# Moving ScalarE's pieces for the turned results, the down half's first cast and the bank copies within their queues, in a one-core decoder layer

## The chip, the cores and the metric

The kernel runs on one core of one Trainium2 chip. The metric is the device time of one execution in microseconds. The core has a matrix engine (TensorE, PE in the profile, its weight loads PEld), VectorE (DVE), ScalarE (ACT), GpSimd (POOL) and SyncE (SP), each with a queue of its own that is worked off in the order in which the program was written; semaphores join the queues. Matmuls write eight banks of PSUM, 512 float32 columns each.

## The reference

One decoder layer for 256 tokens with a model width of 2048, all in float32. The part that this change touches is the feed-forward:

```python
D_FF = -(-8 * D_MODEL // (3 * 256)) * 256          # 5632
...
    f = rmsnorm(h, ffn_norm[i])
    h = h + (jax.nn.silu(f @ w_gate[i]) * (f @ w_up[i])) @ w_down[i]
```

Ahead of it stand the attention of two head groups and their output projection, behind it a gate on per-layer embeddings and the final norm. None of these changes.

## The kernel before

**Splitting.** Every matmul operand is split in two: a high part, which ScalarE makes by a cast (L338, `split_hi`), and a low part, the rest, which VectorE makes by a subtraction (L349, `split_lo`). A product is three matmuls (`three`, L389 to L391): high times high, low times high, high times low. Weights arrive in raw tiles by SyncE's transfers (five buffers, `raw_112` to `raw_2909` in the rows below) and their parts go into places of `ring`, `more` and `most`, which come free when TensorE has read them.

**Stages.** The 5632 columns of the feed-forward are done in five blocks of 1024 and one of 512. For block n there are a gate gn (`gate`), then the first half of the down product of the block before, then the up product un, then the second half of the down product. In this text d2, d3 and d4 are the first halves that follow g2, g3 and g4 (`d20`, `d30`, `d40` in the code). gu5 is the last, short block, and `dl0` the down half behind it.

**Units.** A gate or up product is eight units of 256 weight rows. Seven of them, S0 to S6, are done with seven products in place of eight (`seven`, Strassen's scheme). Such a unit has four turns, each with a job of its own: the first quarter pair ("11 22", 1024 columns wide), the second quarter ("21", 512), the sums "t1 t3" (1024, here called the third quarter) and "t4 t2" (1024, the fourth). The sums are made in the raw tile by VectorE (L348, L351, L352) between the low parts, so the casts of the third and fourth quarter wait for VectorE. In g2 to g4 the order is unit 7 first, then S0 to S6; a down half is four units, each cast at once (2048 columns).

**The gate's end.** In the last unit of a gate ScalarE copies the finished banks into the tile `stage` (`gate_add`, L1027), four copies, and one of Strassen's products into U (L467). The banks go over to the down half behind it, in the order of the copies, so its first matmul waits for the first copy. VectorE adds up U from the other products (L474 to L477), and POOL adds U to `stage` by a transfer (`gate_sum`). At the end of a down half ScalarE copies its banks into `copied` (L945), and the up product's first matmuls take them over.

**The turned results.** `ff_transpose` turns the result of an up product (TensorE at L1065, ScalarE's copies at L1069) into the left operand of the down half that follows the next gate. Its parts are made by `by_transfer`, a task of four pieces during that gate: two high parts by ScalarE's casts (L1089, `ffTh`), then two low parts, each a negated copy by ScalarE (L1092, `ffTl`) and an accumulating transfer that POOL issues (L1093). A task goes a step on at every second turn (`step`).

**What sets the order.** The program is written out by the loop at the end: for each turn of each unit it collects the jobs whose raw tile and place are free by the plan (`todo`), lets `high_parts` write their casts, steps the tasks, writes the low parts and then the matmuls. No scheduler changes this order afterwards.

Of the kernel before, what the change touches and what calls it, by code (L numbers as in the profile page):

```python
# [35 lines left out]
def kernel(ctx, tc, x, w_in, w_ukv, w_o, w_gate, w_up, w_down, w_ple_gate, w_ple_proj,  # L36
                             final_norm, x_turned, p_turned, columns_in, out):
    nc = tc.nc
# [130 lines left out]
    units = []  # L169
# [61 lines left out]
    jobs, turns = [], []  # L231
# [99 lines left out]
    def split_hi(jb, c0=0, c1=None, n=1, row=slice(None)):  # L331

        jb.cast = c1 is None
        h, l, r = (x[:, row] for x in by_row_tile(n, *parts_of(jb), raw_of(jb)))
        if units[jb.unit].adding:
            nc.scalar.mul(l, r, -1.0)
            nc.gpsimd.dma_start(l, r, accum_op=ALU.add)
        nc.scalar.copy(h[:, :, c0:c1], r[:, :, c0:c1])  # L338

    def split_lo(jb, c0=0, c1=None, n=1, row=slice(None)):  # L340

# [104 lines left out]
    def seven(u, turn):  # L446
        st = u.st
        if turn == 0 and u.sevens_first:
            take_banks(u)
            n = B["next"] % 4  # L450
            st["free"] = B["rot"][n:] + B["rot"][:n]
            B["rot"], B["next"] = [st["banks"][1, 1]] if u.first else [], 0
            st.update(zip(("m1", "m7", "m5", "m6"), st["free"]))
        h, l = u.turns[turn][0].h, u.turns[turn][0].l
        k = u.ks[0]
        a11, a12, a22 = u.lhs(k, 0), u.lhs(k + 1, 0), u.lhs(k + 1, 1)
        s1, s2, s3, s4 = (u.sums(k, j) for j in range(4))
        todo = (((0, "m1", a11), (1, "m3", s4)), ((0, "m2", a12),), ((1, "m7", s3), (0, "m5", s1)),
                ((1, "m6", s2), (0, "m4", a22)))[turn]
        alone = {"m2": (0, 0), "m3": (1, 0), "m4": (0, 1)}  # L460
        for q, m, xs in todo:
            b = st["banks"][alone[m]] if m in alone else st[m]
            three(b, xs, h[:, 512 * q:512 * q + 512], l[:, 512 * q:512 * q + 512], begins(u, alone.get(m, m)),
                  u.sevens_end and (u.last or m not in alone))
        if u.sevens_end and turn == (0 if u.last else 3):
            S["U"] = big.tile([128, NT, 1024], F32, name="U", tag="vb")
            nc.scalar.copy(S["U"][:, 0, 0:512], st["m1"])  # L467
        for c, t in (((1, 1), (1, 0)), ((0, 0),), (), ((0, 1),))[turn] if u.last else ():
            u.evac(c, t, *u.chunks[c], st["banks"][c, t])
        if turn == 3 and u.sevens_end:  # L470
            U = S["U"]
            c1, c2 = U[:, :, 0:512], U[:, :, 512:1024]
            tt = nc.vector.tensor_tensor
            tt(c2[:, 0], c1[:, 0], st["m6"], op=ALU.add)  # L474
            tt(c1[:, 1], c2[:, 0], st["m7"], op=ALU.add)
            tt(c2[:, 0], c2[:, 0], st["m5"], op=ALU.add)
            tt(c2[:, 1], c1[:, 1], st["m5"], op=ALU.add)  # L477
            B["rot"], B["next"] = st["free"], 0
            if u.last:
                gate_sum()  # L480
                B["acc"] = [st["banks"][ct] for ct in ((1, 1), (1, 0), (0, 0), (0, 1))]
            if u.into is not None:
                def join(hs=S["h"][:, :, u.into:u.into + 1024]):
                    tt(hs, hs, U, op=ALU.add)
                    yield 1
                add(join())
# [28 lines left out]
    def add(gen, wait=0, front=False):  # L515
        tasks.insert(0 if front else len(tasks), [wait, gen])
# [72 lines left out]
    turn = {"P": 0, "pT": 0}  # L589
# [464 lines left out]
    def ff_transpose(ci, n, st):  # L1054
        if ci == 5:
            ft = big.tile([128, 2, 6, SEQ], F32R, name="ffT", tag="att")
            tl = ffT[ci] = [ft[:, 0], ft[:, 1]]
        else:
            tl = ffT[ci] = parts_tile("ffT", "f0")
        lows = []  # L1060
        for k in range(0, n // 128, 2):
            b = obank()
            for i in range(2):
                for t in range(NT):
                    nc.tensor.transpose(b[:, (2 * i + t) * 128:(2 * i + t + 1) * 128],  # L1065
                                        st[:, t, (k + i) * 128:(k + i + 1) * 128], ident)
            h, l, f = tl[0][:, k:k + 2, :], tl[1][:, k:k + 2, :], b.rearrange("q (a s) -> q a s", a=2)
            if ci in (1, 2, 3, 4):
                nc.scalar.copy(st[:, :, k * 128:(k + 2) * 128], f)  # L1069
            elif ci or k < 4:  # L1070
                split_psum(h, l, f)
            else:
                kept = st[:, :, k * 128:(k + 2) * 128]
                nc.scalar.copy(kept, f)
                lows.append((l, kept, h))
                nc.scalar.copy(h, kept)
            if k % 4 == 2:
                yield 1

        def low_parts():  # L1080
            for l, kept, h in lows:
                nc.vector.tensor_tensor(l, kept, h.bitcast(F32), op=ALU.subtract)
            yield 1

        def by_transfer():
            v = st.rearrange("q a (m s) -> q m a s", s=SEQ)
            h, l = (x.rearrange("q (m a) s -> q m a s", a=2) for x in tl)
            for a in range(2):
                nc.scalar.copy(h[:, :, a], v[:, :, a])  # L1089
                yield 1  # L1090
            for a in range(2):
                nc.scalar.mul(l[:, :, a], v[:, :, a], -1.0)  # L1092
                nc.gpsimd.dma_start(l[:, :, a], v[:, :, a], accum_op=ALU.add)  # L1093
                yield 1
        if lows:
            add(low_parts(), 11, True)
        elif ci < 5:
            add(by_transfer(), 2)

    def ff_l(k, t):  # L1100
        ci, kk = divmod(k, 8)
# [216 lines left out]
    for n in range(3):  # L1318
        for i in range(4):
            if n:  # L1320
                u = Unit()
# [26 lines left out]
        split_lo(jobs[1], c0, c1)  # L1348
    add(prologue(), 1)

    def high_parts(todo):

        ahead = [jb for jb in todo if not (jb.kind in ("t1 t3", "t4 t2") and any(
            x.unit == jb.unit and x.kind in ("11 22", "21") for x in todo))]
        for jb in ahead:
            if not jb.cast:
                split_hi(jb)

# [14 lines left out]
    def may_wait(i, jb):  # L1373
        return i in (end_u0 - 1, end_u0) and (
            jb.unit > end_u0 + 2 or jb.unit == end_u0 + 2 and jb.kind in ("t1 t3", "t4 t2"))

    for i, u in enumerate(units):
# [32 lines left out]
        for n in range(max(1, len(u.turns))):  # L1410
# [3 lines left out]
            while nxt < len(jobs) and jobs[nxt].unit in raw and jobs[nxt].wait < j and jobs[nxt].unit <= i + (3 if i > 1 else 1) and \  # L1414
                    (jobs[nxt].unit <= i + 2 or i >= wide and units[jobs[nxt].unit].asked < i) and \
                    not (u.sevens_end and u.name != "u0" and 0 <= n < 3 and jobs[nxt].unit > i + 1) and \
                    not may_wait(i, jobs[nxt]):
                todo.append(jobs[nxt])
                nxt += 1
            weave = u.name in WOVEN and u.last  # L1420
# [63 lines left out]
```

## Time and profile before

| | |
|---|---|
| median of 3 runs | 1191.82 us (1191.62 to 1191.92) |
| the profiled execution, its own time | 1192.29 us |
| its span, first to last instruction | 1190.3 us |
| mean granted TensorE clock | 0.995 |
| casts of weights into `ring`, `more`, `most` (L338, ACT) | 377.1 + 85.4 + 58.8 us |
| low parts of the same (L349, DVE) | 442.5 + 98.9 + 69.1 us |
| sums in the raw tiles (L348, L352, DVE) | 69.8 + 39.4 us |

The times of one engine add up along its queue; those of different engines lie beside each other. A number in square brackets behind a row of a timeline is the time for which the engine stood idle before it, with what ended this. A row with x3 holds three instructions that follow each other. In the list of waits the numbers are us in all, times, and the longest.

### The profile page before, as it was taken

The page shows a single profiled execution, that of the slowest core. Times are in us where ns is not written, and L with a number is a line of the kernel's source. Part 1 is how long each engine was busy: PE and PEld are TensorE (multiplying, and loading weights), DVE is VectorE, ACT ScalarE, POOL GpSimd, SP SyncE. Part 2 cuts the span into 40 slices and gives each one's busy share as a digit, 9 for nine tenths or more (in the row PEclk, how much of TensorE's full clock was granted, in tenths as well). Part 3 has the DMA queues.
Part 4 walks back from the last instruction along what each step waited for, and adds up shares of the span by engine and source line. Part 5 has one row for each costly group of instructions (what it writes and reads, how often), then busy time and mean ns, then how long its engine had stood idle before and what let it go on. Part 6 is the DMA issues. An engine that isn't in the chain of part 4 may idle for free.

```text
span 1190.3 us, 14715 instructions
## 1 busy us (share of the span) xinstructions
PE 1169.5 (98%) x5459; PEld 975.9 (82%) x5459; DVE 980.4 (82%) x1167; ACT 737.9 (62%) x939; POOL 61.0 (5%) x82
## 2 busy tenths in 40 slices
PE   9999999999999999999999999899989999999996
PEld 7888888899888888888887888688878888888886
DVE  7866656875567779999989998999899989898984
ACT  6745745457466655767666766667576667465563
POOL 5000000000000000000000000000000000000000
PEclk9999999999999999999999999999999999999999
DMA  9896886755675686787978697878778797936441
GB/s 331 284 350 214 289 298 235 277 181 213 242 288 176 241 285 243 270 268 251 303 200 272 187 339 224 248 210 323 235 201 255 262 299 196 376 117 238 155 165 70
DMA packets 90103, 291.99 MB, mean 245 GB/s; under 512 B 5808, under 2 KB 12208, under 8 KB 85424
## 3 DMA queue, kind: packets, MB, share of 16 engines
q1 hardware_dynamic: 76208, 238.66, 55.6%
q0 software_dynamic: 13248, 51.38, 16.7%
q10 hardware_dynamic: 576, 1.02, 0.3%
q8 instruction: 42, 0.69, 0.2%
q14 instruction: 29, 0.24, 0.1%
HBM read 252.24 MB, written 26.21 MB: 234 GB/s over the span
## 4 chain that ended last, share of the span: by engine, by line
PE 92%; DVE 3%; ACT 2%; issue 2%; DMA 0%; ACTq 0%; DVEq 0%; SPq 0%
PE bank L391 29%; PE bank L389 29%; PE bank L390 29%; DVE ringl L349 1%; PE bank L602 1%; PE bank L1065 1%; ACT ringh L338 1%; PE bank L123 1%; ACT moreh L338 1%; PE bank L631 1%; PE bank L625 0%; PE bank L737 0%; PE bank L605 0%; DVE raw L348 0%; DVE raw L352 0%
## 5 line engine op out<-in xcount | busy, mean ns | idle before, releaser
L338 ACT CAST ringh<-raw 128x1024 fp32r<-128x1024 f32 (+4 forms) x322 | 377.1, 1205 | 237.1 <-PE bank L390 82.5
L349 DVE TENSOR_TENSOR ringl<-raw,ringh 128x1024 fp32r<-128x1024 f32 (+5 forms) x319 | 442.5, 1407 | 87.1 <-ACT ringh L338 85.4
L389 PE MATMUL bank<-ringh,aT 128*128 128x512 f32 (+3 forms) x688 | 264.8, 385 | 0.5 <-ACT copied L945 0.5
L391 PE MATMUL bank<-ringl,aT 128*128 128x512 f32 (+3 forms) x688 | 260.8, 379 | 0.1
L390 PE MATMUL bank<-ringh,aT 128*128 128x512 f32 (+3 forms) x688 | 260.4, 378 | 0.0
L389 PEld LDWEIGHTS bank<-ringh,aT 128*128 128x128 f32 x688 | 129.4, 188 | 24.8 <-ACT copied L945 1.3
L391 PEld LDWEIGHTS bank<-ringl,aT 128*128 128x128 f32 x688 | 129.2, 188 | 24.2 <-DVE ringl L349 0.8
L390 PEld LDWEIGHTS bank<-ringh,aT 128*128 128x128 f32 x688 | 129.4, 188 | 22.7 <-DVE aT L669 0.2
L338 ACT CAST moreh<-raw 128x1024 fp32r<-128x1024 f32 (+2 forms) x78 | 85.4, 1127 | 46.0 <-DVE raw L348 29.8
L349 DVE TENSOR_TENSOR morel<-raw,moreh 128x1024 fp32r<-128x1024 f32 (+2 forms) x77 | 98.9, 1304 | 10.8 <-ACT moreh L338 10.2
L338 ACT CAST most<-raw 128x1024 fp32r<-128x1024 f32 (+2 forms) x58 | 58.8, 1036 | 28.7 <-DVE raw L348 15.6
L389 PE MATMUL bank<-ringh,ffTh 128*128 128x512 f32 x180 | 71.0, 394 | 2.0 <-ACT stage L1027 2.0
L348 DVE TENSOR_TENSOR raw<-raw 128x1024 f32<-128x1024 f32 x57 | 69.8, 1225 | 2.0
L349 DVE TENSOR_TENSOR most<-raw,most 128x1024 fp32r<-128x1024 f32 (+2 forms) x58 | 69.1, 1202 | 2.2 <-ACT most L338 1.9
L391 PE MATMUL bank<-ringl,ffTh 128*128 128x512 f32 x180 | 70.8, 393 | 0.0
L390 PE MATMUL bank<-ringh,ffTl 128*128 128x512 f32 x180 | 70.6, 392 | 0.0
L389 PEld LDWEIGHTS bank<-ringh,ffTh 128*128 128x128 f32 x180 | 34.2, 190 | 9.5 <-ACT stage L1027 2.4
L389 PE MATMUL bank<-moreh,aT 128*128 128x512 f32 x105 | 41.3, 393 | 0.0
L352 DVE TENSOR_TENSOR raw<-raw 128x512 f32<-128x512 f32 x57 | 39.4, 692 | 2.0
L391 PE MATMUL bank<-morel,aT 128*128 128x512 f32 x105 | 40.9, 390 | 0.0
L390 PE MATMUL bank<-moreh,aT 128*128 128x512 f32 x105 | 40.9, 389 | 0.0
L390 PEld LDWEIGHTS bank<-ringh,ffTl 128*128 128x128 f32 x180 | 34.2, 190 | 7.1
(379 smaller groups left out, 2053.4 us busy)
## 6 DMA issues: line engine op xcount, KB each, us to landing
raw<-in_w_down SPq DMA_DIRECT2D x44, 1024.0 KB, 6.5
raw<-in_w_gate SPq DMA_DIRECT2D x37, 1024.0 KB, 8.4
raw<-in_w_up SPq DMA_DIRECT2D x30, 1024.0 KB, 5.9
raw<-in_w_in SPq DMA_DIRECT2D x40, 512.0 KB, 5.2
raw<-in_w_o SPq DMA_DIRECT2D x16, 1024.0 KB, 5.9
raw<-in_w_ple_gate SPq DMA_DIRECT2D x16, 1024.0 KB, 5.1
wsums<-in_w_up POOLq DMA_DIRECT2D x10, 1024.0 KB, 7.5
wsumsu<-wsums POOLq DMA_DIRECT2D x10, 1024.0 KB, 4.7
```

Source lines behind the costliest of these rows:

```text
L123: nc.tensor.transpose(b[:, (2 * i + t) * 128:(2 * i + t + 1) * 128], part[:, t, i * 128:(i + 1) * 128], ident)
L338: nc.scalar.copy(h[:, :, c0:c1], r[:, :, c0:c1])
L348: tt(f[:, 0:2], f[:, 1:2].to_broadcast([128, 2, 512]), f[:, 0:4:3], op=ALU.subtract)
L349: tt(l[:, :, c0:c1], r[:, :, c0:c1], h[:, :, c0:c1].bitcast(F32), op=ALU.subtract)
L352: tt(f[:, 2], f[:, 2], f[:, 3], op=ALU.subtract)
L389: nc.tensor.matmul(b, xh, h, start=start, stop=False)
L390: nc.tensor.matmul(b, xl, h, start=False, stop=False)
L391: nc.tensor.matmul(b, xh, l, start=False, stop=stop)
L602: nc.tensor.matmul(s[:, c0:c0 + nk], qT[:, q * 128:(q + 1) * 128], kT[:, 0:nk], start=True, stop=qpe is None)
L631: nc.tensor.matmul(o[:, 0:256], v(0), pT[:, 0:256], start=True, stop=False)
L1065: nc.tensor.transpose(b[:, (2 * i + t) * 128:(2 * i + t + 1) * 128], st[:, t, (k + i) * 128:(k + i + 1) * 128], ident)
```

## The change

```diff
@@ split_hi
         nc.scalar.copy(h[:, :, c0:c1], r[:, :, c0:c1])
+        if jb.kind != "21":
+            return
+        if pieces:
+            pieces.pop(0)()
+
+    pieces = []
@@ seven
-        if u.sevens_end and turn == (0 if u.last else 3):
+        for c, t in (((1, 1), (1, 0)), ((0, 0),), (), ((0, 1),))[turn] if u.last else ():
+            u.evac(c, t, *u.chunks[c], st["banks"][c, t])
+        if u.sevens_end and turn == (1 if u.last else 3):
             S["U"] = big.tile([128, NT, 1024], F32, name="U", tag="vb")
             nc.scalar.copy(S["U"][:, 0, 0:512], st["m1"])
-        for c, t in (((1, 1), (1, 0)), ((0, 0),), (), ((0, 1),))[turn] if u.last else ():
-            u.evac(c, t, *u.chunks[c], st["banks"][c, t])
@@ by_transfer
-            for a in range(2):
-                nc.scalar.copy(h[:, :, a], v[:, :, a])
-                yield 1
-            for a in range(2):
+            def low(a):
                 nc.scalar.mul(l[:, :, a], v[:, :, a], -1.0)
                 nc.gpsimd.dma_start(l[:, :, a], v[:, :, a], accum_op=ALU.add)
-                yield 1
+            def high(a):
+                nc.scalar.copy(h[:, :, a], v[:, :, a])
+            pieces.extend([partial(low, 0), partial(low, 1), partial(high, 0), partial(high, 1)])
...
         elif ci < 5:
-            add(by_transfer(), 2)
+            by_transfer()
@@ the loop
+    def behind_run(i, n=1):
+        return i >= wide and units[i].idx == n - 1 and units[i - n].strassen
+
+    def held(i, jb):
+        u = units[jb.unit]
+        if u.strassen and u.last and jb.kind in ("t1 t3", "t4 t2"):
+            return next(x for x in jobs[nxt:] if x.unit == jb.unit + 1).wait >= j
+        return any(behind_run(jb.unit, n) for n in (2, 3)) and i < jb.unit - 2
@@ high_parts
-        for jb in ahead:
+        for jb in sorted(ahead, key=lambda x: not behind_run(x.unit)):
@@ the loop's condition for a job
-                    not may_wait(i, jobs[nxt]):
+                    not may_wait(i, jobs[nxt]) and not held(i, jobs[nxt]):
```

The four pieces of the turned results are no longer a task: each is written right behind the next cast of a second quarter, the low ones first. The third and fourth quarter of a gate's last unit are held back until the first unit of the down half has its place by the plan, and that unit's cast is written ahead of theirs; the casts of the second and third unit of the down half are held back until two units ahead. In the last unit the bank copies are written before the copy to U, which goes a turn later. The order on TensorE, on POOL and on SyncE is the same as before, and no instruction is added or taken away.

ScalarE's queue in g3 where S4 (`raw3`) and S5 (`raw4`) are cast. Before:

```order
L338 CAST ringh_115<-raw3_2907 128x1024
L338 CAST ringh_115<-raw3_2907 128x512
L1092 ACTIVATE ffTl_5082<-stage_4519 128x4x256
L338 CAST ringh_115<-raw3_2907 128x1024 x2
L1092 ACTIVATE ffTl_5082<-stage_4519 128x4x256
L338 CAST ringh_115<-raw4_2909 128x1024
L338 CAST ringh_115<-raw4_2909 128x512
L338 CAST ringh_115<-raw4_2909 128x1024
```

With the change:

```order
L338 CAST ringh_115<-raw3_2907 128x1024
L338 CAST ringh_115<-raw3_2907 128x512
L1100 CAST ffTh_5081<-stage_4514 128x4x256
L338 CAST ringh_115<-raw3_2907 128x1024 x2
L338 CAST ringh_115<-raw4_2909 128x1024
L338 CAST ringh_115<-raw4_2909 128x512
L1100 CAST ffTh_5081<-stage_4514 128x4x256
L338 CAST ringh_115<-raw4_2909 128x1024
```

The piece between S4's fourth quarter and S5's first has gone behind S5's second quarter; the two low pieces have moved up to S2 and S3.

ScalarE's queue at the end of g3: S6 (`raw0`), then the four units of d3 (`raw1` to `raw4`). Before:

```order
L338 CAST most_3392<-raw0_112 128x512
L338 CAST most_3392<-raw0_112 128x1024
L338 CAST ringh_115<-raw0_112 128x1024
L338 CAST ringh_115<-raw1_113 128x2048
L338 CAST ringh_115<-raw2_114 128x2048
L467 COPY U_5320<-bank0_77 128x512
L1027 COPY stage_5322<-bank5_82 128x512
L1027 COPY stage_5322<-bank7_84 128x512
L1027 COPY stage_5322<-bank6_83 128x512
L338 CAST moreh_2523<-raw3_2907 128x2048
L1027 COPY stage_5322<-bank4_81 128x512
L338 CAST most_3392<-raw4_2909 128x2048
```

With the change:

```order
L338 CAST most_3392<-raw0_112 128x512
L338 CAST ringh_115<-raw1_113 128x2048
L338 CAST most_3392<-raw0_112 128x1024
L338 CAST ringh_115<-raw0_112 128x1024
L1033 COPY stage_5317<-bank5_82 128x512
L1033 COPY stage_5317<-bank7_84 128x512
L1033 COPY stage_5317<-bank6_83 128x512
L475 COPY U_5324<-bank0_77 128x512
L338 CAST ringh_115<-raw2_114 128x2048
L1033 COPY stage_5317<-bank4_81 128x512
L338 CAST moreh_2523<-raw3_2907 128x2048
L338 CAST most_3392<-raw4_2909 128x2048
```

The cast of d3's first unit now stands behind S6's second quarter, and the second unit's cast behind the copies.

VectorE's queue at the same place. Before:

```order
L349 TENSOR_TENSOR most_3392<-raw0_112,most_3392 128x1024
L349 TENSOR_TENSOR ringl_116<-raw0_112,ringh_115 128x1024
L349 TENSOR_TENSOR ringl_116<-raw1_113,ringh_115 128x2048
L349 TENSOR_TENSOR ringl_116<-raw2_114,ringh_115 128x2048
L349 TENSOR_TENSOR morel_2524<-raw3_2907,moreh_2523 128x2048
L474 TENSOR_TENSOR U_5320<-U_5320,bank3_80 128x512
```

With the change:

```order
L355 TENSOR_TENSOR most_3392<-raw0_112,most_3392 128x1024
L355 TENSOR_TENSOR ringl_116<-raw0_112,ringh_115 128x1024
L355 TENSOR_TENSOR ringl_116<-raw1_113,ringh_115 128x2048
L355 TENSOR_TENSOR ringl_116<-raw2_114,ringh_115 128x2048
L480 TENSOR_TENSOR U_5324<-U_5324,bank3_80 128x512
L481 TENSOR_TENSOR U_5324<-U_5324,bank2_79 128x512
```

The sums of U stand ahead of the low part of d3's third unit instead of behind it; the order of the other low parts is kept.

## The prediction, made before the change was run

> **What bounds the kernel now.** I read the busy shares first, then TensorE's waits, then the stretches round those waits engine by engine.
>
> ```profile
> PE 1169.5 (98%) x5459; PEld 975.9 (82%) x5459; DVE 980.4 (82%) x1167; ACT 737.9 (62%) x939; POOL 61.0 (5%) x82
> ```
>
> TensorE is busy for 98% of the span, so reordering can bring little over one per cent. What can be had lies where it stands still, and the list of its waits has one cause at the top: three waits of 2.0 us for ScalarE's copies out of the banks (L1027).
>
> ```profile
> PE bank L389 <- ACT stage L1027: 6.0, 3, 2.0
> ```
>
> They stand at the ends of the gates g2, g3 and g4. TensorE's timeline at the end of g3:
>
> ```profile
> 757.16 0.50 PE L391 MATMUL bank<-most,sums6h 128*128 128x512 f32 x1 [1.17 <-DVE most L349]
> ...
> 761.76 0.50 PE L389 MATMUL bank<-ringh,ffTh 128*128 128x512 f32 x1 [2.02 <-ACT stage L1027]
> ```
>
> First it waits for VectorE's low part of the third quarter of S6 (the gate's last unit), then for a bank that d3 wants. Right behind, the clock falls (granted clock is the third number from the end); in g4 it doesn't:
>
> ```profile
> 763.04:766.44 3.40, 3.40 (x10) 2.66 (x9) 2.36 (x2) 3.40 (x3) 0.00 (x0) 0.50 0.98 384
> ...
> 885.89:889.30 3.41, 2.43 (x10) 1.65 (x10) 2.82 (x2) 3.41 (x3) 0.00 (x0) 1.00 0.33 56
> 889.30:892.70 3.40, 2.36 (x10) 1.97 (x11) 2.75 (x2) 3.40 (x6) 0.00 (x0) 1.00 1.00 376
> ```
>
> 3.4 us at half speed lose 1.7 us behind g3, and as much behind g2. In g4 the same wait of 2.0 us is spread over two of these stretches, and nothing is lost.
>
> Why does the low part come late? VectorE's timeline, and ScalarE's below it:
>
> ```profile
> 744.82 1.23 DVE L349 TENSOR_TENSOR ringl<-raw,ringh 128x1024 fp32r<-128x1024 f32 x1 [0.67 <-ACT ringh L338]
> ...
> 750.42 2.36 DVE L349 TENSOR_TENSOR morel<-raw,moreh 128x1024 fp32r<-128x1024 f32 x2
> 752.82 1.23 DVE L348 TENSOR_TENSOR raw<-raw 128x1024 f32<-128x1024 f32 x1
> ...
> 755.89 1.22 DVE L349 TENSOR_TENSOR most<-raw,most 128x1024 fp32r<-128x1024 f32 x1
> 757.16 1.23 DVE L349 TENSOR_TENSOR ringl<-raw,ringh 128x1024 fp32r<-128x1024 f32 x1
> 758.98 4.50 DVE L349 TENSOR_TENSOR ringl<-raw,ringh 128x2048 fp32r<-128x2048 f32 x2 [0.59 <-ACT ringh L338]
> 764.52 2.29 DVE L349 TENSOR_TENSOR morel<-raw,moreh 128x2048 fp32r<-128x2048 f32 x1 [1.04 <-ACT moreh L338]
> ```
>
> ```profile
> 742.79 1.06 ACT L1092 ACTIVATE ffTl<-stage 128x1024 fp32r<-128x1024 f32 x1
> 743.75 1.56 ACT L338 CAST ringh<-raw 128x1024 fp32r<-128x1024 f32 x2
> ...
> 751.24 0.62 ACT L338 CAST most<-raw 128x512 fp32r<-128x512 f32 x1
> 754.16 1.05 ACT L338 CAST most<-raw 128x1024 fp32r<-128x1024 f32 x1 [2.29 <-DVE raw L348]
> 756.09 4.66 ACT L338 CAST ringh<-raw 128x1024 fp32r<-128x1024 f32 x3 [0.88 <-DVE raw L352]
> 760.64 0.58 ACT L467 COPY U<-bank 128x512 f32<-128x512 f32 x1
> 761.12 1.56 ACT L1027 COPY stage<-bank 128x512 f32<-128x512 f32 x3
> ```
>
> Between its bracketed gaps VectorE works without a break: it is **the engine that sets the end of each gate**. A gap of 0.67 arises where ScalarE does a piece for the turned results (1.06 us, L1092) just ahead of the next unit's first cast. The gaps of 0.59 and 1.04 arise because d3's casts come late, the latter behind the bank copies.
>
> **The change part by part.** It adds and removes no instruction, and no DMA: everything is a move on ScalarE, with one on VectorE.
>
> The **pieces** now stand behind the second-quarter cast. There ScalarE waits anyhow: 2.29 us ahead of 754.16 in the row above, for VectorE's L348. A piece of 1.06 us fits in it, so the two gaps of 0.67 in g3 close. The two low pieces go first, so POOL's two accumulating transfers are issued earlier, which nobody waits for; the high ones are done at least a unit ahead of their first use.
>
> The **first cast of d3** goes ahead of S6's third-quarter cast. Moved earlier by 2 x 0.65 us, S6's second-quarter cast ends at 751.86 - 1.35 = 750.5; the moved cast takes 1.9 (the row at 756.09 holds 1.05 and two of these) and ends at 752.4; L348 ends at 754.05 - 1.3 = 752.75. The cover is 0.35 us: later than that, every microsecond of this cast delays VectorE's next low part by one.
>
> The **bank copies** then follow the fourth-quarter cast directly: that cast ends near 755.9, so d3's first bank is free at 756.4 instead of 761.7. The wait of 2.02 goes. What is late next is VectorE: S6's third-quarter low part is ready at 757.1 - 1.3 = 755.8. TensorE wants it at about 755.2 (757.16 less the 1.17 idle and some 0.8 of holds too short for the list), so 0.6 to 0.7 of that wait stays; S6's fourth follows, and d3's first low part (2.29) is ready at 759.4 where TensorE wants it at 758.6: a new wait of 0.8. Then the second d3 cast ends at 759.6, a gap of 0.2 on VectorE, and the **sums of U** go ahead of the third low part, which has time (d3's third unit is 11 us behind its first).
>
> So TensorE could go 2.85 us earlier (d3's third matmul, the one that reads the low part, stood at 762.3 and now at 759.5), and 1.7 more if the clock stays up: 4.5. But VectorE only gains its closed gaps, and ScalarE's casts for u3 follow it. The same rows for the other gates, as sums of waits in 34 and 33 us round their ends, g2 first, then g4:
>
> ```profile
> DVE ringl L349 <- ACT ringh L338: 1.7, 2, 1.1
> DVE most L349 <- ACT most L338: 0.7, 1, 0.7
> DVE morel L349 <- ACT moreh L338: 0.6, 1, 0.6
> ```
>
> ```profile
> DVE ringl L349 <- ACT ringh L338: 1.7, 2, 1.1
> DVE morel L349 <- ACT moreh L338: 0.6, 1, 0.6
> ```
>
> VectorE gains in g2 1.7 + 0.7 + 0.6 - 0.3 = 2.7; in g3 2 x 0.67 + 0.59 + 1.04 - 0.3 = 2.65; in g4 1.7 + 0.6 - 0.4 = 1.9 (only one piece's gap there; the 0.2 to 0.4 is what stays at the second cast). At the end of each down half stands the next check: the copy of its first bank (L945) comes behind casts that follow VectorE, and the next unit wants that bank. ScalarE's copy at d2's end, and TensorE's first matmuls behind d2, d3 and d4:
>
> ```profile
> 654.64 1.55 ACT L945 COPY copied<-bank 128x512 f32<-128x512 f32 x3
> ```
>
> ```profile
> 656.15 0.39 PE L389 MATMUL bank<-ringh,aT 128*128 128x512 f32 x1
> ```
>
> ```profile
> 785.37 0.50 PE L389 MATMUL bank<-ringh,aT 128*128 128x512 f32 x1
> ```
>
> ```profile
> 912.96 0.50 PE L389 MATMUL bank<-ringh,aT 128*128 128x512 f32 x1 [0.55 <-ACT copied L945]
> ```
>
> Behind d2 the copy is done at 655.2, 0.95 before it is wanted; behind d3 it just holds TensorE (a matmul of 0.50 is one that waited), behind d4 it does by 0.55. With the copies earlier by VectorE's gain alone, TensorE gains there at most 2.7 + 0.95 = **3.6** (it could 4.3), **2.65** (it could 4.5: a new wait of 1.9 for L945), **1.9** (it could 2.0). In gu5 two pieces' gaps close likewise, and a hold of 0.2 goes. The sum is 3.6 + 2.65 + 1.9 + 0.2 = **8.3 us**. The u units behind start with VectorE's lead as before: after d3 and d4 both engines move by the same amount; after d2 TensorE moves 0.9 further, which can cost a part of this in u2.
>
> The clock: half of it followed single waits of 2.0 us inside one stretch of 3.4 (g2, g3) and not 1.2 us in one. The new wait of 1.9 lies between. I take no halving, since it must also fall inside one stretch; the other end is 1.7 us. The Trainium skill (TensorE: Matmul & The Clock Gate, "Part 1: The HAM clock gate") lets the clock fall only after an idle window of about 3.4 us. The trace disagrees: waits of 2.0 us were enough. By the trace the halvings go with these waits; by the Trainium skill's rule they had another cause and would stay.
>
> **The rivals.**
>
> *VectorE isn't what sets the pace* behind the gates, and no wait for L945 arises: then TensorE has all that it could gain, 4.3 + 4.5 + 2.0 + 0.2 = 11.0, 1180.8. For it speaks that TensorE's own rows show these losses; against it VectorE's unbroken work from 744.8 to 758.4, and the 0.55 for L945 that is there already.
>
> *Halved clock comes back* behind the new 1.9 us wait: 8.3 - 1.7 = 6.6, 1185.2. Near half of the places at which the wait can fall would put it into one stretch; whether 1.9 is enough no row says.
>
> *The halvings aren't these waits' doing* and stay: that behind g3 hides in the new wait for L945, that behind g2 costs 1.7 less the 0.7 that it hides there, 7.3 in all, 1184.5. Against it: two of two stand right behind a wait of 2.0 in one stretch. The Trainium skill's page on the clock gate would have it so.
>
> *Pieces bring nothing*, as another wait (TensorE's release of ring places) keeps VectorE's gaps: then only the tails count, 0.6 + 1.05 - 0.3 = 1.3 a gate, and 0.95: 3 x 1.3 + 0.95 = 4.9, 1186.9.
>
> *Slower*: the moved cast waits for its place in the ring, or for its load, at the head of ScalarE's queue, with S6's third and fourth casts and the bank copies behind it. Beyond 0.35 us it costs one for one, in three gates; it eats the gain at 0.35 + 8.3 / 3 = 3.1 us, and at 4 us the kernel ends near 1194. Against it stand the issue of that load in g3 and the last matmul that reads the place, in g3, g2 and g4:
>
> ```profile
> 729.93 14.61 SPq L221 DMA_DIRECT2D raw<-in_w_down  x3
> ```
>
> ```profile
> 747.48 0.39 PE L391 MATMUL bank<-ringl,aT 128*128 128x512 f32 x1
> ```
>
> ```profile
> 619.79 0.39 PE L391 MATMUL bank<-morel,aT 128*128 128x512 f32 x1
> ```
>
> ```profile
> 878.19 0.39 PE L391 MATMUL bank<-morel,sumsmore_sums 128*128 128x512 f32 x1
> ```
>
> The load is issued 20 us before the cast, and the places are free 2.6, 1.2 and 1.1 us before it (cast at 750.5; by the same shifts 621.4 and 879.7).
>
> *Nothing happens*: the moves shift waits alone and VectorE's own durations rise; within 0.2%.
>
> **How the numbers follow.** The profiled execution took 1192.29, 0.47 above the median of 1191.82; minus 8.3 it is 1184.0, and against the median 1183.5. Chances: forecast 0.60 (1182 to 1185), halved clock back 0.10, halvings stay 0.04, pieces bring nothing 0.10, VectorE not the pace 0.06, nothing 0.05, slower 0.05. The range from 1180.5 to 1187.3 takes in the first five but for their edges, somewhat over eight in ten. A measurement of this kernel tells 0.2% (2.4 us) from no change: faster 0.90, same 0.05, slower 0.05.
>
> **What would show it.** Right: the L1027 waits gone from TensorE's list; VectorE's gaps of 0.67 in g2 to g4 gone; L945 up to about 3 us in all, as TensorE's largest wait; new waits under 1 us for d's first low part; clock 1.00 behind g2 and g3. Wrong: a gap on VectorE ahead of S6's third quarter (the cover of 0.35 is too thin); or no wait for L945 at d3's end, which means VectorE wasn't what set the pace.

## The result, and the profile after

The changed kernel takes 1182.84 us (median of 4 runs, 1182.67 to 1183.92) against 1191.87 us before (4 runs, 1191.62 to 1192.23). The ratio is 0.9926 with a 95% interval from 0.9909 to 0.9943: 9.0 us less. The profiled execution of the changed kernel took 1182.74 us, its span is 1181.0 us and its mean granted clock 0.998.

TensorE does the same instructions in the same order, and it still waits in a few places. The page's line of busy times, then the list of TensorE's waits (us in all, times, longest). The lines of the source have moved by six, so L389 to L391 are now L395 to L397, L349 is L355, L945 is L951 and L1027 is L1033.

```profile
PE 1164.6 (99%) x5459; PEld 973.8 (82%) x5459; DVE 979.3 (83%) x1167; ACT 737.8 (62%) x939; POOL 61.3 (5%) x82
```

```profile
PE bank L395 <- ACT copied L951: 3.2, 3, 1.7
...
PE bank L397 <- DVE ringl L355: 0.9, 2, 0.5
PE bank L397 <- DVE most L355: 0.5, 1, 0.5
PE bank L397 <- DVE morel L355: 0.4, 1, 0.4
```

The three waits of 2.0 for the bank copies of a gate have gone from the list altogether. In their place stand the copies at the end of the down halves, 3.2 in all, and four short waits for low parts. TensorE's timeline at d2's end, at the end of g3, and at the ends of d3 and d4:

```profile
652.21 0.50 PE L395 MATMUL bank<-ringh,aT 128*128 128x512 f32 x1 [0.74 <-ACT copied L951]
...
751.87 0.50 PE L397 MATMUL bank<-most,sums6h 128*128 128x512 f32 x1 [0.49 <-DVE most L355]
...
754.27 0.39 PE L395 MATMUL bank<-ringh,ffTh 128*128 128x512 f32 x1
...
755.28 0.50 PE L397 MATMUL bank<-ringl,ffTh 128*128 128x512 f32 x1 [0.39 <-DVE ringl L355]
...
778.60 0.50 PE L395 MATMUL bank<-ringh,aT 128*128 128x512 f32 x1 [1.72 <-ACT copied L951]
...
903.96 0.50 PE L395 MATMUL bank<-ringh,aT 128*128 128x512 f32 x1 [0.72 <-ACT copied L951]
```

The first matmul of d3 (754.27) stood at 761.76 before, with a wait of 2.02. The matmuls behind d2, d3 and d4 stood at 656.15, 785.37 and 912.96: TensorE has gained 3.94, 6.77 and 9.00 us by then, so 3.94 in g2, 2.83 in g3 and 2.23 in g4, each counted to the first matmul behind the down half. VectorE's timeline at the end of g3, then ScalarE's:

```profile
745.13 2.36 DVE L355 TENSOR_TENSOR morel<-raw,moreh 128x1024 fp32r<-128x1024 f32 x2
747.52 1.23 DVE L354 TENSOR_TENSOR raw<-raw 128x1024 f32<-128x1024 f32 x1
...
750.60 1.22 DVE L355 TENSOR_TENSOR most<-raw,most 128x1024 fp32r<-128x1024 f32 x1
751.79 3.43 DVE L355 TENSOR_TENSOR ringl<-raw,ringh 128x1024 fp32r<-128x1024 f32 x2
755.55 2.29 DVE L355 TENSOR_TENSOR ringl<-raw,ringh 128x2048 fp32r<-128x2048 f32 x1 [0.33 <-ACT ringh L338]
757.76 0.68 DVE L480 TENSOR_TENSOR U<-U,bank 128x512 f32<-128x512 f32 x1
```

```profile
742.03 1.05 ACT L338 CAST ringh<-raw 128x1024 fp32r<-128x1024 f32 x1 [1.26 <-DVE raw L354]
...
746.47 1.91 ACT L338 CAST ringh<-raw 128x2048 fp32r<-128x2048 f32 x1
748.78 1.05 ACT L338 CAST most<-raw 128x1024 fp32r<-128x1024 f32 x1 [0.41 <-DVE raw L354]
750.72 1.05 ACT L338 CAST ringh<-raw 128x1024 fp32r<-128x1024 f32 x1 [0.88 <-DVE raw L358]
751.67 1.56 ACT L1033 COPY stage<-bank 128x512 f32<-128x512 f32 x3
753.10 0.61 ACT L475 COPY U<-bank 128x512 f32<-128x512 f32 x1
753.58 1.94 ACT L338 CAST ringh<-raw 128x2048 fp32r<-128x2048 f32 x1
```

VectorE shows one gap, 0.33 ahead of d3's second low part, where before there were 0.67, 0.67, 0.59 and 1.04. The moved cast of d3 (746.47) takes 1.91 of the time in which ScalarE used to wait 2.29 for VectorE; 0.41 of that wait is left (748.78).

The clock fell nowhere in the feed-forward of this execution. The longest wait, 1.72 from 776.88 to 778.60, lies wholly in one of the stretches of 3.41 us by which the clock is granted (the first four numbers of a row: us, then busy time of PE, PEld and DVE; the third from the end is the granted clock):

```profile
776.23:779.64 3.41, 1.69 (x8) 1.05 (x7) 3.32 (x4) 3.41 (x6) 0.00 (x0) 1.00 0.10 19
779.64:783.05 3.41, 3.41 (x16) 2.81 (x15) 3.03 (x4) 3.41 (x5) 1.10 (x1) 1.00 0.95 316
```

TensorE was busy for 1.69 of 3.41, and the next stretch kept its clock of 1.00.

### The profile page after: what moved, and what is told of

It reads as the page before. It is cut to its first block, busy times and chain, and to the rows that moved or that the text cites. A ratio compares the mean times of both kernels' runs of the same rounds, so it can differ in the third digit from the quotient of the medians.

```text
span 1181.0 us, 14701 instructions
## 1 busy us (share of the span) xinstructions
PE 1164.6 (99%) x5459; PEld 973.8 (82%) x5459; DVE 979.3 (83%) x1167; ACT 737.8 (62%) x939; POOL 61.3 (5%) x82
## 3 DMA queue, kind: packets, MB, share of 16 engines
q10 hardware_dynamic: 576, 1.02, 0.3%
## 4 chain that ended last, share of the span: by engine, by line
PE 89%; DVE 6%; issue 3%; ACT 2%; DMA 0%; DVEq 0%; ACTq 0%; SPq 0%
PE bank L397 28%; PE bank L395 28%; PE bank L396 28%; DVE ringl L355 2%; PE bank L608 1%; PE bank L1071 1%; DVE raw L358 1%; DVE most L355 1%; DVE raw L357 1%; PE bank L123 1%; PE bank L637 1%; DVE raw L354 1%; DVE morel L355 0%; ACT moreh L338 0%; PE bank L611 0%
## 5 line engine op out<-in xcount | busy, mean ns | idle before, releaser
L355 DVE TENSOR_TENSOR ringl<-raw,ringh 128x1024 fp32r<-128x1024 f32 (+5 forms) x319 | 441.8, 1407 | 80.6 <-ACT ringh L338 75.8
L395 PE MATMUL bank<-ringh,aT 128*128 128x512 f32 (+3 forms) x688 | 264.7, 385 | 3.5 <-ACT copied L951 3.2
L397 PE MATMUL bank<-ringl,aT 128*128 128x512 f32 (+3 forms) x688 | 260.8, 379 | 0.1
L395 PEld LDWEIGHTS bank<-ringh,aT 128*128 128x128 f32 x688 | 129.3, 188 | 27.7 <-ACT copied L951 4.5
L397 PEld LDWEIGHTS bank<-ringl,aT 128*128 128x128 f32 x688 | 129.2, 188 | 24.2 <-DVE ringl L355 0.8
L355 DVE TENSOR_TENSOR morel<-raw,moreh 128x1024 fp32r<-128x1024 f32 (+2 forms) x77 | 98.9, 1304 | 9.0 <-ACT moreh L338 8.4
L355 DVE TENSOR_TENSOR most<-raw,most 128x1024 fp32r<-128x1024 f32 (+2 forms) x58 | 69.1, 1202 | 2.8 <-ACT most L338 2.5
L397 PE MATMUL bank<-ringl,ffTh 128*128 128x512 f32 x180 | 70.2, 390 | 0.4 <-DVE ringl L355 0.4
L395 PE MATMUL bank<-ringh,ffTh 128*128 128x512 f32 x180 | 70.1, 390 | 0.0
L395 PE MATMUL bank<-moreh,aT 128*128 128x512 f32 x105 | 41.3, 393 | 0.0
L397 PE MATMUL bank<-morel,aT 128*128 128x512 f32 x105 | 40.9, 390 | 0.0
L397 PEld LDWEIGHTS bank<-ringl,ffTh 128*128 128x128 f32 x180 | 33.8, 188 | 7.8 <-DVE ringl L355 0.8
```

The source lines that it names most:

```text
L355: tt(l[:, :, c0:c1], r[:, :, c0:c1], h[:, :, c0:c1].bitcast(F32), op=ALU.subtract)
L395: nc.tensor.matmul(b, xh, h, start=start, stop=False)
L397: nc.tensor.matmul(b, xh, l, start=False, stop=stop)
```

## The experiments

Nine kernels were run. "Before" is measured again on the chip of each group: 1192.43 (first four), 1191.95 (next three), 1192.04 (last two).

| what it is | us | ratio to before, interval |
|---|---|---|
| pieces alone | 1187.56 | 0.9958 [0.9943, 0.9972] |
| the change without the pieces | 1187.00 | 0.9955 [0.994, 0.9969] |
| the change without the casts' move | 1187.20 | 0.9957 [0.9942, 0.9972] |
| the change with U copied first | 1182.91 | 0.9919 [0.9903, 0.9936] |
| the change, down half's copies between casts | 1178.56 | 0.9886 [0.987, 0.9902] |
| the change, U copied last | 1181.52 | 0.9914 [0.9901, 0.9927] |
| both of these | 1178.53 | 0.9887 [0.9872, 0.9903] |
| copies between casts, one cast ahead of the turned results | 1175.81 | 0.9865 [0.985, 0.9881] |
| copies between casts, without the pieces | 1182.86 | 0.9925 [0.9912, 0.9938] |

### The pieces alone

The kernel before, with only this:

```diff
         nc.scalar.copy(h[:, :, c0:c1], r[:, :, c0:c1])
+        if jb.kind != "21":
+            return
+        if pieces:
+            pieces.pop(0)()
...
-            add(by_transfer(), 2)
+            by_transfer()
```

> The kernel before with the pieces alone moved; casts and bank copies in the old order. My theory (VectorE's pace, copies behind it): VectorE's gaps of 0.67 to 0.77 behind pieces go, two in g2, three in g3 (one of them at the changeover, not counted before), one in g4, two in gu5; the waits of 2.0 for the bank copies at the ends of g2 to g4 stay as long as they are, only earlier. Gain by the terms of the prediction 8.3 - 4.9 = 3.4, so 1188.4; up to 4.3 (1187.5) if the earlier waits happen to fall across two clock stretches and a halving goes. Rival (pieces bring nothing): 1191.8. Rival (VectorE isn't the pace, TensorE's own losses count): TensorE's waits for S6's third quarter alone shrink, by 0.6 to 1.2 in three gates, 1188.8 as well, but then VectorE's gaps would reappear elsewhere in the same gate.

It took 1187.56 (1187.25 to 1187.64), 4.9 less than before on the same chip. The time is the upper end of what was expected (1187.5), and the reason named there holds: one halving is left of two, as only one of the waits for the bank copies fell into a single stretch of the clock. Behind g2 that wait is 1.39, where 2.0 was expected. TensorE's waits of this kernel, and the stretches around the ends of g3 and g4:

```profile
PE bank L395 <- ACT stage L1033: 5.4, 3, 2.0
PE bank L395 <- ACT copied L951: 2.1, 2, 1.6
```

```profile
752.85:756.26 3.41, 2.59 (x10) 1.80 (x10) 2.77 (x3) 3.41 (x3) 0.00 (x0) 1.00 0.18 23
756.26:759.67 3.41, 1.74 (x8) 1.44 (x9) 3.38 (x2) 3.41 (x6) 0.00 (x0) 1.00 0.95 341
882.56:885.97 3.41, 1.40 (x7) 0.85 (x6) 2.99 (x2) 3.41 (x5) 0.00 (x0) 1.00 0.72 208
885.97:889.38 3.41, 3.41 (x9) 2.64 (x9) 2.37 (x2) 3.41 (x5) 0.00 (x0) 0.50 1.02 375
```

The wait of 2.00 behind g3 is now spread over two stretches (busy 2.59 and 1.74), and the clock stays. The wait of 2.01 behind g4 lies in one (busy 1.40), and half the clock follows there, where the kernel before had none. So the pieces' gaps count, and the rival in which they bring nothing is out. The other rival, TensorE's own losses, gave 1188.8, too near to VectorE's 1188.4 to be told apart by the time. But in it VectorE's gaps come up again elsewhere in the gate, and between 723 and the end of g3 there is none; the 0.58 and 1.05 at the end are those of the kernel before.

### The change without the pieces

The changed kernel with `pieces` and its call taken out of `split_hi` and the task `by_transfer` put back, in `add(by_transfer(), 2)`.

> The changed kernel with the pieces back in their old places; first cast and bank copies ahead as in the change. My theory: the tails alone bring 1.3 a gate plus the 0.95 that d2's copies have to spare, 4.9 in all, so 1187.0; the waits for the bank copies are gone, the clock stays at 1.00, the waits for L945's copies at the ends of d3 and d4 grow beyond those of the changed kernel (1.72 and 0.72) since VectorE is later, and the gaps of 0.67 ahead of first quarters are back. Rival (pieces bring nothing): as the changed kernel, 1182.8. Rival (tails bring nothing): 1191.8.

It took 1187.00, as expected to the tenth, though one of the waits behind that number came out otherwise. TensorE's waits (this kernel has the old line numbers):

```profile
PE bank L389 <- ACT copied L945: 3.1, 3, 1.7
PE bank L391 <- DVE ringl L349: 2.3, 3, 1.3
...
PE bank L391 <- DVE most L349: 1.2, 1, 1.2
```

The bank copies of the gates are gone from the list, and the waits for S6's third quarter are back, at 0.62, 1.24 and 1.25 in g2, g3 and g4. One point was wrong: the waits for L945 did not grow beyond those of the changed kernel. They are the same 3.1, because TensorE, held at S6's third quarter, is later by as much as VectorE: 3.18 at the first matmul of d3, where the matmul that the copies release behind d3 is 3.19 later.

Pieces alone and tails alone (the moves at a gate's end) bring 4.9 and 5.4, together 10.3, where the whole (the run with U copied first, on the same chip) brings 9.5. By the starts behind d2 the parts bring 2.45 and 2.30 and the whole 3.94, and these 0.8 are near the 0.95 that d2's copies had to spare, which each part takes and which is there only once. By the end of the kernel the traces differ by only 0.2 (4.45 and 5.03 against 9.28), as the pieces alone lose 0.9 to the halving behind g4. The 0.8 of the medians is little more than the 0.6 by which before's own medians differ (1192.43 here, 1191.87 above), so the time alone does not carry this account.

### The casts' move taken back

```diff
-        for jb in sorted(ahead, key=lambda x: not behind_run(x.unit)):
+        for jb in ahead:
...
-                    not may_wait(i, jobs[nxt]) and not held(i, jobs[nxt]):
+                    not may_wait(i, jobs[nxt]):
```

> The changed kernel with the casts of the down half back behind S6's fourth quarter (and so ahead of the bank copies); pieces moved, U copied behind the bank copies. My theory: VectorE's gaps of 0.6 and 1.05 at each gate's end return, TensorE's waits for the bank copies return at 1.5 (2.0 less the 0.5 that the copy to U took ahead of them), the clock stays at 1.00 because a wait of 1.5 is shorter than the 1.72 that left it at 1.00 in the changed kernel. Gain over before: 2.2 behind g2 (1.3 of VectorE and 0.95), 1.4 behind g3, 0.7 behind g4, 0.2: 4.5, so 1187.3. Rival (the place of the bank copies alone counts, not the casts): they stand behind the casts again, so this says the same for the copies; but if VectorE's gaps cost nothing, TensorE loses only the 1.5 in three gates against the changed kernel, less what its waits for the copies at the end of the down halves (0.74, 1.72, 0.72) take back: 1184.4.

This also puts VectorE's sums of U back behind the third low part. It took 1187.20, where VectorE's theory said 1187.3 and the rival 1184.4. TensorE's waits:

```profile
PE bank L395 <- ACT copied L951: 4.1, 3, 2.0
PE bank L395 <- ACT stage L1033: 4.0, 3, 1.5
```

The bank copies hold TensorE again, by 0.91, 1.55 and 1.54 (1.5 in each was expected), and VectorE's gaps of 0.59 and 1.05 are back. The wait of 2.04 for `copied` behind d3 lay across two stretches, and the clock stayed at 1.00.

### U copied first

```diff
+        if u.sevens_end and turn == (0 if u.last else 3):
+            S["U"] = big.tile([128, NT, 1024], F32, name="U", tag="vb")
+            nc.scalar.copy(S["U"][:, 0, 0:512], st["m1"])
         for c, t in (((1, 1), (1, 0)), ((0, 0),), (), ((0, 1),))[turn] if u.last else ():
             u.evac(c, t, *u.chunks[c], st["banks"][c, t])
-        if u.sevens_end and turn == (1 if u.last else 3):
-            S["U"] = big.tile([128, NT, 1024], F32, name="U", tag="vb")
-            nc.scalar.copy(S["U"][:, 0, 0:512], st["m1"])
```

> The changed kernel with the copy to U back ahead of the bank copies of a gate's last unit; casts and pieces as in the change. My theory: nothing, 1182.8 within 0.3: the first bank copy then ends near 752.7 in g3, where TensorE wants the bank only at 754.27. Rival (this part of the change carries the lost wait of 2.0 for the bank copies): 0.5 in each of three gates, 1184.3.

1182.91 against 1182.84: nothing. This part of the change is idle by itself. What brings the bank copies forward is that the down half's first two casts no longer stand between S6's fourth quarter and them; the 0.5 for U fits, since TensorE is not at these banks before 754.27.

### The down half's copies between the casts, and U copied last

The waits of 3.2 that the change left behind are for copies that stand on ScalarE behind two casts, which wait for VectorE. Here the first copy goes ahead of the first of these casts and the second copy ahead of the second:

```diff
-                if between and (c, t) == u.order[0]:
+                if between and (c, t) in u.order[:2]:
                     split(between.pop(0))
...
+            behind = []
+            if u.name in ("d20", "d30", "d40") and u.last:
+                behind, todo = todo, []
...
-                product(..., late if weave else ())
+                product(..., late if weave else behind)
```

> The changed kernel with the copies at the end of d2, d3 and d4 written between the last two casts of that unit (first bank, cast, second bank, cast, third and fourth bank) instead of behind both; nothing else moved. The first copy then fits into a stretch in which ScalarE waits 2.3 (d2, d4) or 0.95 (d3) for VectorE. TensorE's waits for these copies (0.74, 1.72, 0.72: 3.2 in all) go. Theory A, as in the prediction (VectorE sets the pace, and the copies only show it): TensorE's lead on VectorE is spent at once at the next place where its low parts are just in time, at the end of u2 (0.27 to spare), g4 (0.05) and u4 (0.06); new waits there, no gain beyond 0.5, 1182.3 to 1182.8. Theory B (VectorE itself waits for TensorE behind each of these places, 1.66 behind d2 and d4 for a place in the ring and 2.1 and 2.3 ahead of g4, so it moves along): nearly all 3.2 come, 1179.6 to 1180.3, and TensorE's waits at the ends of the next units stay as they are.

It took 1178.56, 4.3 less than the changed kernel, more than either theory gave; theory A is out. ScalarE's timeline at d2's end in this kernel:

```profile
647.51 0.59 ACT L951 COPY copied<-bank 128x512 f32<-128x512 f32 x1 [1.00 <-PE bank L397]
648.79 1.05 ACT L338 CAST ringh<-raw 128x1024 fp32r<-128x1024 f32 x1 [0.69 <-DVE raw L354]
649.75 0.58 ACT L951 COPY copied<-bank 128x512 f32<-128x512 f32 x1
650.66 1.05 ACT L338 CAST ringh<-raw 128x1024 fp32r<-128x1024 f32 x1 [0.33 <-DVE raw L358]
651.61 1.07 ACT L951 COPY copied<-bank 128x512 f32<-128x512 f32 x2
```

The copies fit beside the waits for VectorE (0.69 and 0.33 of them are left), and TensorE's first matmuls behind d2, d3 and d4 follow without a bracket:

```profile
651.39 0.39 PE L395 MATMUL bank<-ringh,aT 128*128 128x512 f32 x1
...
775.74 0.39 PE L395 MATMUL bank<-ringh,aT 128*128 128x512 f32 x1
...
900.07 0.39 PE L395 MATMUL bank<-ringh,aT 128*128 128x512 f32 x1
```

They come 0.82, 2.86 and 3.89 earlier than in the changed kernel, and the next units keep it. Why VectorE isn't in the way is in its timeline right behind d2, first of the changed kernel, then of this one:

```profile
654.60 1.23 DVE L355 TENSOR_TENSOR ringl<-raw,ringh 128x1024 fp32r<-128x1024 f32 x1 [1.66 <-PE bank L397]
```

```profile
653.66 1.23 DVE L355 TENSOR_TENSOR ringl<-raw,ringh 128x1024 fp32r<-128x1024 f32 x1 [0.69 <-ACT ringh L338]
```

VectorE stood there for 1.66 until TensorE had read a place of the ring; when TensorE comes earlier, so does VectorE. Behind d4 it is the same, with 1.67. Behind d3, where the most is gained, VectorE waited for a cast of ScalarE instead:

```profile
783.59 1.23 DVE L355 TENSOR_TENSOR most<-raw,most 128x1024 fp32r<-128x1024 f32 x1 [0.88 <-ACT most L338]
```

That cast comes later in ScalarE's queue than the copies. With the copies between the casts this gap is gone, one of 0.21 is new ahead of it, and a gap of 0.98 at the end of u3 falls to 0.18; the rest of the lead comes out of a gap of 2.13 at the start of g4, which falls to 1.41. The size was set too low: by the starts of the matmuls around them, the listed waits of 0.74, 1.72 and 0.72 had cost TensorE 1.05, 2.01 and 1.02, about 0.3 more each, and another 0.2 came at the end of u4, where a low part had just held it in the changed kernel (a hold too short for the list). That is 4.3.

The second edit sends the copy to U to the end of the gate's last unit, behind the down half's second cast:

```diff
-        if u.sevens_end and turn == (1 if u.last else 3):
+        if u.sevens_end and turn == 3:
```

> The changed kernel with the copy to U in a gate's last unit moved behind the second cast of the down half and the fourth bank copy. VectorE's gap of 0.33 ahead of the second low part goes in g2, g3 and g4. Theory A (VectorE's pace, the copies at the end of the down half behind it): these copies come 0.33 earlier in each, 1.0 in all, 1181.8. Theory B (something else sets the time of these copies): 1182.8.

1181.52, where theory A said 1181.8 and B 1182.8. The copies at the end of the down halves do follow VectorE as long as they stand behind its casts: TensorE's wait for them falls from 3.2 to

```profile
PE bank L395 <- ACT copied L951: 1.9, 3, 1.3
```

Both edits together:

> The two edits of the runs before it together. Theory A: TensorE gains only what VectorE does, 1.0 and up to 0.5, 1181.3 to 1181.8. Theory B: 3.2 from the copies, and VectorE's 0.33 in three gates add lead that TensorE's waits at the ends of g3 and g4 (0.4 to 0.5) take at most once: 1178.6 to 1180.

1178.53, just what the copies alone gave. This is at theory B's lower edge, but the part of it on VectorE's lead is wrong: with the copies out of the way, VectorE's 0.33 at the start of a down half is worth nothing, and TensorE's waits at the ends of g3 and g4 (0.5 and 0.4) are as they were.

### One cast ahead of the turned results

In g3 and g4 one more cast follows TensorE where it need not: the first-quarter cast of the gate's third unit stands behind the four copies of the turned result. The two rows of ScalarE and the row of VectorE in the kernel with the copies between the casts:

```profile
715.29 2.06 ACT L1075 COPY stage<-bank 128x512 f32<-128x512 f32 x4 [0.57 <-PE bank L1071]
717.21 1.08 ACT L338 CAST ringh<-raw 128x1024 fp32r<-128x1024 f32 x1
```

```profile
718.32 1.23 DVE L355 TENSOR_TENSOR ringl<-raw,ringh 128x1024 fp32r<-128x1024 f32 x1 [2.27 <-ACT ringh L338]
```

```diff
                 while late and (u.name != "g1" or units[i + 1].early and late[0].unit == i + 1):
                     split(late.pop(0))
+                if u.name in ("g3", "g4") and jobs[nxt].kind == "11 22" and jobs[nxt].wait == j and jobs[nxt].unit in raw:
+                    split(jobs[nxt])
+                    nxt += 1
                 for _ in S.pop("mid"):
```

> The kernel with the copies at a down half's end between the casts (the run of 1178.56), and one more cast moved: in g3 and g4 the first-quarter cast of the third unit goes ahead of the four copies of the turned result (L1075), behind which VectorE waits 2.3 for it. TensorE in g3 and g4 still waits 0.5 for S6's third quarter and 0.4 for the down half's first low part. If VectorE's lead is what these waits lack (inside a gate VectorE sets the pace): it gains 0.8 or more (ScalarE's low piece still stands ahead of the next cast), the two waits go in both gates, 1.0 to 1.2 each with the restart, so 1176.2 to 1176.8, and nothing is lost again at the end of d3 and d4. If VectorE's lead is not what they lack: 1178.5.

1175.81, 2.75 less, a little more than expected, as each wait again cost more than its bracket; TensorE's list of waits is empty behind the kernel's first microseconds. VectorE's gap of 2.27 is gone (its three low parts now run on, behind a gap of 0.70):

```profile
713.15 3.50 DVE L355 TENSOR_TENSOR ringl<-raw,ringh 128x1024 fp32r<-128x1024 f32 x3 [0.70 <-ACT ringh L338]
```

So inside a gate VectorE's lead is what TensorE's waits lack, as the prediction had it. This version is 16.2 us faster than before on the same chip, and 7.0 below the changed kernel's median of another group.

### Copies between casts, without the pieces

The run of the change without the pieces, with the edit of `product` and `behind` from above.

> The changed kernel without its pieces (the run of 1187.0), with the copies at a down half's end between the casts. Theory A (VectorE's lost time adds up from gate to gate): the pieces are worth what they were with the copies in the old place, 4.2, so 1178.56 + 4.2 = 1182.8. Theory B (each down half resets VectorE's lead, since VectorE waits there for TensorE): only what TensorE waits longer inside each gate, 0.6 in g2 and 0.75 in g3 and g4 for S6's third quarter, and 0.2 in gu5: 2.3, so 1180.9.

1182.86: the pieces are worth 4.3 here, 4.2 with the copies in the old place. That is theory A's number, and theory B's 2.3 is wrong; but not because lost time is carried over. VectorE's gaps and TensorE's waits at the end of g3 in this kernel:

```profile
733.91 1.23 DVE L349 TENSOR_TENSOR ringl<-raw,ringh 128x1024 fp32r<-128x1024 f32 x1 [0.67 <-ACT ringh L338]
741.42 1.23 DVE L349 TENSOR_TENSOR ringl<-raw,ringh 128x1024 fp32r<-128x1024 f32 x1 [0.67 <-ACT ringh L338]
```

```profile
753.77 0.50 PE L391 MATMUL bank<-most,sums6h 128*128 128x512 f32 x1 [1.25 <-DVE most L349]
...
757.18 0.50 PE L391 MATMUL bank<-ringl,ffTh 128*128 128x512 f32 x1 [0.35 <-DVE ringl L349]
```

Against the kernel with the pieces, TensorE loses 1.56 in g2, 1.54 in g3, 0.77 in g4, 0.2 in u4 and 0.5 in gu5 (by the starts of its matmuls), all inside these stages, and nothing at the ends of the down halves. Theory B had counted the listed waits for the third quarter alone. It left out holds that are too short for the list (0.4 and 0.4 in g3, ahead of 753.77), 0.65 for the first low part of the down half behind g2, 0.3 by which the third quarter of g2 costs more than its bracket, the 0.2 in u4, and most of gu5.

## Why the prediction was right, point by point

The forecast was 1183.5, the time is 1182.84. The gain of 9.0 has the parts that were forecast, and in the places named.

- **The pieces fit into ScalarE's waits**: right. The gaps of 0.67 in the gates are gone; undone, this costs 4.2 us.
- **The first cast has a cover of 0.35**: right, 0.41, 0.41 and 0.40 are left of ScalarE's wait in g2, g3 and g4. The prediction writes the shift ahead of this cast as 2 x 0.65 and reckons with 1.35, which is 2 x 0.67. Longer delays were not tried.
- **The bank copies' wait of 2.0 goes**: right in the three gates. By the runs it is the casts' move that does it; once the casts are moved, the order of U and the bank copies makes no difference.
- **What is late next**: right in kind. The wait for S6's third quarter is 0.49 and 0.50 (forecast 0.6 to 0.7), for the down half's first low part 0.39 and 0.39 in g3 and g4 (0.8); in g2, for which no number was given, neither is there. The gap at the second cast is 0.33 (0.2 to 0.4).
- **L945 limits TensorE at the end of the down halves**: right, with waits of 0.74 and 1.72 behind d2 and d3, where 0.7 and 1.9 followed from the forecast, and 0.72 behind d4; 3.2 in all where about 3 was said.
- **The sum**: 3.6, 2.65, 1.9 and 0.2 were forecast; TensorE gained 3.94, 2.83, 2.23 and 0.27. Each term is somewhat small. The last is 0.5 in gu5, less 0.2 at the end of u4, where a low part now holds TensorE, which the forecast didn't have. The terms added up bracketed idle times, and closing one brings more than the bracket: two low parts in a row take 2.36 us, one behind a gap 1.23, so 0.10 less together than apart. A closed gap of 0.67 brought 0.75 to 0.79 by VectorE's starts, and at the end of d2 VectorE was 3.05 earlier, where 2.7 was forecast.
- **The clock**: right, but in part by luck. No halving came behind the wait of 1.72, so the rival in which it came back, with a chance of 0.10, is out. The reason that was given, that the wait must also fall inside one stretch, is not what decided: it did fall inside one, and was short enough. A wait of the forecast's 1.9 in one stretch would leave 1.5 us of work there, which no trace has. The rival in which the halvings were not these waits' doing is out by the run with the pieces alone: the halving moved to g4, with the one wait of 2.0 that fell into a single stretch. The Trainium skill (TensorE: Matmul & The Clock Gate, "Part 1: The HAM clock gate") calls the window free-running, which agrees with that; its idle window of about 3.4 us before the clock falls does not agree with a stretch that had 1.40 us of work in it.
- **u2 might give back a part of 0.9**: it did not. The matmuls that follow the one that waited come 3.74 earlier, and TensorE kept this through u2 and into g3, since VectorE, which waits for TensorE behind d2, moved along.
- **"VectorE sets the pace"**: right inside the gates, wrong behind the down halves, though this cost the forecast nothing. TensorE was held at L945 because the copies stand behind two casts in ScalarE's queue that follow VectorE. That is a place in a queue and no limit of VectorE's: with the copies between the casts TensorE gained 4.3 more. The rival "VectorE isn't the pace" gave 1180.8; the changed kernel stays 2 us above it, and it takes the copies between the casts to get below.

## What to carry to other kernels

Look for engines that wait at the head of their queue for one producer while work that needs nothing stands behind them: a cast, a copy or a piece that fits into the wait is free there, and what it used to hold up comes earlier by the time for which it was held. When a change removes one wait, the next in line shows how far the gain goes; ask of that one too whether it is a true limit or only a place in a queue. Price a gap by the starts of the instructions on both sides, where the bracket alone is too small.

## What the runs showed of the hardware

The granted clock changes at the edges of stretches of 3.41 us. In the kernel before it is half from 633.33 to 636.74 and from 763.04 to 766.44; the two starts lie 129.71 apart, 38 times 3.413. In the changed kernel, where it falls only at the end of the program, at 1175.59, the edge at 776.23 lies 117 such stretches ahead of that. The record of the clock begins at such an edge, 4.65 to 7.65 us behind the first instruction in the eleven traces, so the stretches lie differently against the program in each. In the kernel before, the stretch with the wait behind g2 and the next one, and the stretch with the wait behind g3 (the prediction shows the one that follows it):

```profile
629.90:633.32 3.42, 1.42 (x7) 0.85 (x6) 3.42 (x2) 3.42 (x5) 0.00 (x0) 1.00 0.84 266
633.33:636.74 3.41, 3.41 (x10) 2.64 (x9) 2.36 (x2) 3.41 (x4) 0.00 (x0) 0.50 1.00 383
759.63:763.03 3.40, 1.38 (x7) 1.05 (x6) 3.40 (x2) 3.40 (x6) 0.00 (x0) 1.00 0.97 316
```

With 1.38 to 1.42 us of work of TensorE in a stretch the next one had half the clock (three times, the third in the run with the pieces alone); with 1.69 and 1.74 it kept all of it. Counted stretch by stretch, as far as the record of the clock goes, none of the eleven traces has an exception: all with 1.42 or less are followed by half, none with 1.69 or more is, and none lies between. The same wait of 2.0 us cost a halving or none, by where it fell: in the kernel before it did behind g2 and g3 and not behind g4, with the pieces alone behind g4 and not behind g3. Where the limit between 1.42 and 1.69 lies, and whether it counts busy time or something else, was not tried.

A wait of TensorE costs some 0.3 us more than its bracket. Matmuls that follow each other start 0.23 apart and take 0.39, so 0.16 of the one before is hidden, and a wait ends that; and the matmul behind the wait takes 0.50, with the next one starting 0.34 behind it (778.60 and 778.94 behind the wait of 1.72). The starts are what counts here: the ends of matmuls are modelled in these profiles.
